# A two-layer diffusion backbone: row norms of the MLP summed in two halves, and low parts moved to another engine

## The chip, the cores and the metric

The kernel runs on one core of one Trainium2 chip. The metric is the device time of one execution in microseconds. The core's engines run side by side and are tied by semaphores: TensorE (PE in the profile) multiplies and transposes, VectorE (DVE) and ScalarE (ACT) work on tiles and read the accumulators, GpSimd (POOL) works on tiles in the core's memory, SyncE (SP) issues most loads.

## The reference

Two trunk layers work on 512 latent tokens and, in the first layer only, on 256 context tokens, all of width 1024. The part that the change touches is the second half of each layer:

```python
mix = concatenate([pool_mixer(...), gla_output(...), attention(...)]) @ w_out
x = x + ga1 * mix
x = x + ga2 * squared_relu_mlp(rmsnorm(x, g_mlp) * (1 + sc2) + sh2, w_up, w_down)

def rmsnorm(x, g):
    return x * rsqrt(mean(x * x, axis=-1) + 1e-6) * g
def squared_relu_mlp(h, w_up, w_down):
    return square(relu(h @ w_up)) @ w_down
```

The context tokens do the same with their own modulation. All is float32; a second norm of the same kind opens the next layer.

## The kernel before, in words

Every product is made of three fp32r passes: each operand is split into a high part (rounded) and a low part (the rest), and high x high, low x high and high x low are summed. Weights are loaded (`raw`), rounded on ScalarE (`whi`, line 159) and subtracted on VectorE (`wlo`, line 78). Tokens lie in tiles of 128 rows; two tiles are a pair. Layer 0 has six tiles (pairs 0 and 1 latent, pair 2 context), layer 1 four (pairs 0 and 1).

Behind the mixers a layer goes through the output projection (`op`, `tm_matmul`, line 335). Its first 512 columns are made for all tiles; each result is scaled on VectorE (`rtmp`, line 1157) and added to the residual `X` on GpSimd (line 1158). Then come the second 512 columns pair by pair, added to `X` on VectorE. While pair p is projected, `norm_pair(p-1)` norms the pair before:

- ScalarE squares the whole row of 1024 and sums it (line 270, a scratch write into `xn`), GpSimd makes rstd from the sum in two tiny steps (lines 252 and 253), VectorE scales the row into `xn` (line 280);
- TensorE transposes `xn` in blocks of 128 (line 287) into `ptr` banks, four blocks in one bank: column blocks k and k+1 of both tiles;
- per column block k (0 to 7) ScalarE writes the modulated high part `h2h` (line 295), VectorE or, for k = 1 and 5, ScalarE writes the same in full (`full`, lines 299 and 297), and the low part `h2l` is full less high (line 300): on GpSimd for even k, on VectorE for odd k.

The last pair is normed inside the first block of the MLP: `fm_pair` (line 325) multiplies the first column groups (two in layer 0, four in layer 1) pair by pair, the last pair's norm stands ahead of its own `fm_pair`. After that the up projection runs over whole token rows (`fm_matmul`, lines 316 and 318), `relu` on ScalarE and its square on VectorE follow, and the down projection (`dn`, line 335) comes a block of 512 hidden columns later. In layer 0 the MLP carries the modulation sums of layer 1 with it: weights `rawm` are loaded (line 222) and accumulated into `macc`, the first on ScalarE (line 226), the others on VectorE (line 228). At the end of layer 0 the same `norm_pair` makes the input `hT` of layer 1.

The pools decide much of the timing. The tag "full" has two buffers, "xn" has two (the `macc` tiles take theirs from this tag too). The order on each engine isn't written by hand: the tile framework simulates the program and fixes one static order for each engine, so an edit in one place moves instructions in others.

```python
xn = bp.tile([128, D], F32, tag=tag, name=nm(tag), bufs=2)
ss = mp.tile([128, 1], F32, tag="ss", name=nm("ss"))
A.activation(xn, xt, AF.Square, accum_out=ss)
...
full = bp.tile([128, 512], F32, tag="full", name=nm("full"), bufs=2)
...
(V if kk else G).tensor_tensor(lo, f, hi.bitcast(F32), ALU.subtract)
```

Of the kernel before, what the change touches and what calls it, by code (L numbers as in the profile page):

```python
# [10 lines left out]
F32 = mybir.dt.float32  # L11
F32R = mybir.dt.float32r
I32 = mybir.dt.int32
AF = mybir.ActivationFunctionType
ALU = mybir.AluOpType
AX = mybir.AxisListType

D = 1024
# [5 lines left out]
EPS = 1e-6  # L24
# [10 lines left out]
def hybrid_kernel(ctx, tc, x, c, cx, c_ctx, w_mod, b_mod, g_mix, w_in, w_pool, s_pool, w_gate, b_gate,  # L35
                  g_gla, g_q, g_k, w_out, g_mlp, w_up, w_down, g_final, k_mask, k_rope, k_edge, k_invw, out):
    nc = tc.nc
    V, A, G, T = nc.vector, nc.scalar, nc.gpsimd, nc.tensor

    const = ctx.enter_context(tc.tile_pool(name="const", bufs=1))  # L40
    lay = ctx.enter_context(tc.tile_pool(name="lay", bufs=1))
    wp = ctx.enter_context(tc.tile_pool(name="wp", bufs=5))
    sp = ctx.enter_context(tc.tile_pool(name="sp", bufs=29))
    mp = ctx.enter_context(tc.tile_pool(name="mp", bufs=2))
# [7 lines left out]
    def nm(s):  # L52
        uid[0] += 1
        return f"{s}_{uid[0]}"

    def slot(s, dt=F32, w=NT):
        return sp.tile([128, w], dt, tag="S", name=nm(s))
# [10 lines left out]
    def psA(s):  # L68
        return pa.tile([128, 1024], F32, tag="pa", name=nm(s))

    def psB(s):
        return pb.tile([128, 512], F32, tag="pb", name=nm(s))
# [21 lines left out]
    mhalf = const.tile([128, 1], F32, name="mhalf")  # L94
# [172 lines left out]
    def norm_rows(xt, tag="xn"):  # L267
        xn = bp.tile([128, D], F32, tag=tag, name=nm(tag), bufs=2)
        ss = mp.tile([128, 1], F32, tag="ss", name=nm("ss"))
        A.activation(xn, xt, AF.Square, accum_out=ss)  # L270
        return xn, rstd_of(ss, D, "rstd")

    def norm_pair(p2, X, hT, sc, sh, psf):

        pair = (2 * p2, 2 * p2 + 1)
        s = 0 if p2 < 2 else 1
        xns = []
        for t in pair:
            xn, r = norm_rows(X[t])
            V.tensor_scalar(xn, X[t], r, None, ALU.mult)  # L280
            xns.append(xn)
        col = pair[0] * 128
        for k2 in range(0, KT, 2):
            ps = psf("ptr")
            for kk in range(2):
                for i, xn in enumerate(xns):
                    T.transpose(ps[:, kk * 256 + i * 128:kk * 256 + (i + 1) * 128],
                                xn[:, (k2 + kk) * 128:(k2 + kk + 1) * 128], ident)
            full = bp.tile([128, 512], F32, tag="full", name=nm("full"), bufs=2)
            for kk in range(2):  # L290
                k = k2 + kk
                hi, lo = hT[k][0][:, col:col + 256], hT[k][1][:, col:col + 256]
                p_, f = ps[:, kk * 256:(kk + 1) * 256], full[:, kk * 256:(kk + 1) * 256]
                sc_, sh_ = sc[s][:, k:k + 1], sh[s][:, k:k + 1]
                A.activation(hi, p_, AF.Identity, scale=sc_, bias=sh_)
                if kk and k2 % 4 == 0:
                    A.activation(f, p_, AF.Identity, scale=sc_, bias=sh_)
                else:
                    V.tensor_scalar(f, p_, sc_, sh_, ALU.mult, ALU.add)
                (V if kk else G).tensor_tensor(lo, f, hi.bitcast(F32), ALU.subtract)  # L300

    def new_hT(s):
        return [(slot(s + "h", F32R), slot(s + "l", F32R)) for _ in range(KT)]
# [16 lines left out]
    def fm_pair(ps, wk, hT, nk, p2):  # L320

        cs = slice(p2 * 256, p2 * 256 + 256)
        for k in range(nk):
            for i, (a, b) in enumerate(passes(*wk(k), *hT[k])):
                T.matmul(ps[:, cs], a, b[:, cs], start=(k == 0 and i == 0), stop=(k == nk - 1 and i == 2))  # L325
# [91 lines left out]
    X = None  # L417
    MODS = [None, None]
    for l in range(2):
# [3 lines left out]
        live = alltiles if both else lat_tiles  # L423
# [4 lines left out]
        hT = hT1 if l else new_hT("hT")  # L428
        if l == 0:
            xstack = ExitStack()  # L430
            bp = xstack.enter_context(tc.tile_pool(name="np", bufs=1))
# [712 lines left out]
        bp = xstack.enter_context(tc.tile_pool(name=f"bp{l}", bufs=1))  # L1144
        X, XP = {}, {}
# [7 lines left out]
        def out_res(t, cb, ps):  # L1153

            sl = slice(cb * 512, (cb + 1) * 512)
            tmp = bp.tile([128, 512], F32, tag="rtmp", name=nm("rtmp"), bufs=2)
            V.tensor_tensor(tmp, ps, ga[0 if t < 4 else 1][:, sl], ALU.mult)
            (V if cb else G).tensor_tensor(X[t][:, sl], X[t][:, sl], tmp, ALU.add)
# [3 lines left out]
        for t in live:  # L1162
            ps = psB("op")
            tm_matmul(ps, t, wk, mixT, KT)
            out_res(t, 0, ps)
        h2 = new_hT("h2")
        msc, msh = [scT[:, 1, s] for s in range(2)], [shT[:, 1, s] for s in range(2)]
        wk = wcols(w_out[l], 512, 512, 4)
        for p2 in range(np_):
            ps = psA("op")  # L1170
            for i in range(2):
                tm_matmul(ps[:, i * 512:(i + 1) * 512], 2 * p2 + i, wk, mixT, KT)
                if p2 and i == 0:
                    norm_pair(p2 - 1, X, h2, msc, msh, psB)
                out_res(2 * p2 + i, 1, ps[:, i * 512:(i + 1) * 512])


# [32 lines left out]
        for b in range(NB):  # L1210
            act = []
            for i in range(4):
                nj = 2 if both else 4
                if b == 0 and i < nj:
                    if i == 0:
                        wks = [wcols(w_up[l], j * 128, 128, 1) for j in range(nj)]
                        pss = [psA("up") for j in range(2)]
                        if nj > 2:
                            pss = [p_[:, h * 512:h * 512 + 512] for p_ in pss for h in range(2)]
                        for p2 in range(np_):  # L1220
                            if p2 == np_ - 1:
                                norm_pair(p2, X, h2, msc, msh, psB)
                            for j in range(nj):
                                fm_pair(pss[j], wks[j], h2, KT, p2)
                    ps = pss[i]
                else:
                    wk = wcols(w_up[l], b * 512 + i * 128, 128, 1)
                    ps = psA("up")
                    fm_matmul(ps, wk, h2, KT, True, both)
                r_ = slot("relu")  # L1230
                A.activation(r_[:, 0:N_], ps[:, 0:N_], AF.Relu)  # L1231
                if b % 2 and i < 2:
                    w_ = wide("a", F32R)
                    ah, al = w_[:, 0:NT], w_[:, NT:2 * NT]
                else:
                    ah, al = slot("ah", F32R), slot("al", F32R)
                V.tensor_tensor(r_[:, 0:N_], r_[:, 0:N_], r_[:, 0:N_], ALU.mult)
                A.activation(ah[:, 0:N_], r_[:, 0:N_], AF.Copy)
                sub_lo(al[:, 0:N_], r_[:, 0:N_], ah[:, 0:N_])
                act.append((ah, al))  # L1240
                next(mods, None)
            if pend is not None:
                down(*pend)
            pend = (act, b)
        run(mods)
        if both:
            next_w = [wcols(w_in[1], c0, 128, 2, sl=True) for c0 in (256, 512)]
            hT1 = new_hT("hT")
            msc, msh = [MODS[1][1][:, 0, s] for s in range(2)], [MODS[1][2][:, 0, s] for s in range(2)]

            def after(t):
                if t in (2, 4, 5):
                    norm_pair((2, 4, 5).index(t), X, hT1, msc, msh, psB)

            down(*pend, after)
        else:

            gf = bp.tile([128, D], F32, tag="ga", name="gf", bufs=2)
            nc.scalar.dma_start(gf, g_final.partition_broadcast(128))
            halves = [slice(0, 512), slice(512, 1024)]  # L1260

            def after(t):
                y0, y1 = slot("y", w=512), slot("y", w=512)
                ss = mp.tile([128, 2], F32, tag="ssf", name=nm("ssf"))
                sq = bp.tile([128, 512], F32, tag="full", name=nm("sqf"), bufs=2)
                c0, c1 = halves
                for h, cs in enumerate(halves):
                    A.activation(sq, X[t][:, cs], AF.Square, accum_out=ss[:, h:h + 1])
                G.tensor_tensor(y0, X[t][:, c0], gf[:, c0], ALU.mult)
                G.tensor_tensor(ss[:, 0:1], ss[:, 0:1], ss[:, 1:2], ALU.add)  # L1270
                r = rstd_of(ss[:, 0:1], D, "rstd")
                A.activation(y0, y0, AF.Copy, scale=r)
                nc.scalar.dma_start(out[0, t * 128:(t + 1) * 128, c0], y0)
                V.scalar_tensor_tensor(y1, X[t][:, c1], r, gf[:, c1], ALU.mult, ALU.mult)
                nc.sync.dma_start(out[0, t * 128:(t + 1) * 128, c1], y1)

            down(*pend, after)

    xstack.close()
# [54 lines left out]
```

## Time and profile before

| | |
|---|---|
| median of three runs | 1677.33 us (1676.63 to 1677.76) |
| the profiled execution | 1673.25 us, its span 1671.5 us |
| granted TensorE clock, mean | 0.987 |
| TensorE busy | 1596.4 us (96%) |
| VectorE busy | 919.9 us (55%) |
| ScalarE busy | 632.4 us (38%) |
| GpSimd busy | 411.9 us (25%) |

A start in the trace is counted from the beginning of the span. The window 425 to 465 us holds the norms of pairs 1 and 2 of layer 0, 975 to 1022 the boundary between the layers, 1290 to 1340 the last norm and the first MLP block of layer 1. Instructions of one kind that follow each other are merged in a timeline row (x2 is two of them, and the time is that of both). A wait row says which engine waited, at which line, for whom, and for how long. The granted clock is 1.00 at 2.4 GHz and 0.50 at 1.2 GHz; a number between is a stretch that had both.

### The profile page before, as it was taken

Reading aid. Unit: us, or ns where it says so; the run is one execution under the profiler, and the core shown is the slowest. Engines: PE = TensorE matmul, PEld = TensorE weight load, DVE = VectorE, ACT = ScalarE, POOL = GpSimd, SP = SyncE. Lnnn points to the kernel's source line nnn. Section 1 sums busy time; section 2 is a strip of 40 time slices with the busy share of each in tenths; the row PEclk is TensorE's granted clock in tenths of the full one; section 3 lists DMA queues with packets and bytes.
Section 4 is the critical chain, followed back from the end, with each engine's and each line's share of the span. In section 5 each row is a group of like instructions: output and inputs, shape, how many; then the busy total and the mean of one; then the engine's idle time right before and its main releaser. Section 6 shows DMA issues by size and latency. Waiting matters only on the chain.

```text
span 1671.5 us, 27433 instructions
## 1 busy us (share of the span) xinstructions
PE 1596.4 (96%) x11403; PEld 1305.1 (78%) x11403; DVE 919.9 (55%) x1326; ACT 632.4 (38%) x1078; POOL 411.9 (25%) x484
## 2 busy tenths in 40 slices
PE   7999979899999999999999999897999899999997
PEld 4888756678888888888888889785667888888885
DVE  4437665753673654636446553587763645445554
ACT  5544445661531312213123234455662523223332
POOL 1121311212303041230321462242101122222225
PEclk9999989999999999999999999998999999999999
DMA  9445400222340422515324332100032313333321
GB/s 327 131 127 178 153 2 1 103 89 63 101 139 26 140 97 61 176 48 174 139 76 170 104 108 80 40 2 2 24 124 81 114 51 101 101 101 101 101 101 51
DMA packets 136636, 163.31 MB, mean 98 GB/s; under 512 B 9908, under 2 KB 108608, under 8 KB 136512
## 3 DMA queue, kind: packets, MB, share of 16 engines
q1 hardware_dynamic: 130176, 148.41, 27.9%
q10 hardware_dynamic: 5824, 13.12, 2.2%
q8 instruction: 89, 1.46, 0.4%
q14 instruction: 35, 0.29, 0.1%
q0 software_dynamic: 512, 0.03, 0.0%
HBM read 157.31 MB, written 4.23 MB: 97 GB/s over the span
## 4 chain that ended last, share of the span: by engine, by line
PE 84%; DVE 5%; ACT 4%; DMA 2%; issue 2%; POOL 2%; SPq 0%; ACTq 0%; POOLq 0%; DVEq 0%
PE dn L335 25%; PE up L316 19%; PE tm L335 7%; PE op L335 6%; PE up L318 5%; PE fm L316 4%; PE av L1066 3%; PE pT L1049 2%; PE up L325 2%; PE fm L318 2%; PE sc L1028 1%; PE att L764 1%; PE sc L1029 1%; PE pm L190 1%; DVE nmx L1031 1%
## 5 line engine op out<-in xcount | busy, mean ns | idle before, releaser
L159 ACT ACTIVATE whi<-raw 128x1024 fp32r<-128x1024 f32 (+2 forms) x182 | 185.1, 1031 | 567.2 <-PE dn L335 292.6
L1189 POOL TENSOR_TENSOR X<-X,rtmp 128x512 f32<-128x512 f32 x158 | 216.4, 1372 | 636.0 <-DVE rtmp L1188 635.7
L78 DVE TENSOR_TENSOR wlo<-raw,whi 128x1024 fp32r<-128x1024 f32 (+2 forms) x182 | 223.8, 1238 | 214.8 <-ACT whi L159 212.5
L1188 DVE TENSOR_TENSOR rtmp<-dn,ga 128x512 f32<-128x512 f32 x160 | 109.4, 688 | 215.4 <-PE dn L335 212.2
L335 PE MATMUL dn<-whi,ah 128*128 128x512 f32 x480 | 187.3, 390 | 0.0
L335 PE MATMUL dn<-whi,al 128*128 128x512 f32 x480 | 187.2, 390 | 0.0
L335 PE MATMUL dn<-wlo,ah 128*128 128x512 f32 x480 | 186.4, 390 | 0.0
L316 PE MATMUL up<-h2h,whi 128*128 128x512 f32 x464 | 182.5, 393 | 1.5 <-ACT relu L1231 1.5
L316 PE MATMUL up<-h2h,wlo 128*128 128x512 f32 x464 | 183.0, 394 | 0.0
L316 PE MATMUL up<-h2l,whi 128*128 128x512 f32 x464 | 182.7, 394 | 0.0
L335 PEld LDWEIGHTS dn<-whi,ah 128*128 128x128 f32 x480 | 90.1, 188 | 20.2 <-DVE rtmp L1188 0.8
L335 PEld LDWEIGHTS dn<-whi,al 128*128 128x128 f32 x480 | 90.1, 188 | 19.5
L316 PEld LDWEIGHTS up<-h2h,whi 128*128 128x128 f32 x464 | 87.1, 188 | 23.3 <-ACT relu L1231 1.7
L335 PEld LDWEIGHTS dn<-wlo,ah 128*128 128x128 f32 x480 | 90.1, 188 | 19.1
L316 PEld LDWEIGHTS up<-h2l,whi 128*128 128x128 f32 x464 | 87.1, 188 | 21.7 <-issue 2.5
L335 PE MATMUL tm<-whi,hTh 128*128 128x256 f32 (+1 forms) x352 | 102.2, 291 | 1.0 <-ACT UV L886 1.0
L316 PEld LDWEIGHTS up<-h2h,wlo 128*128 128x128 f32 x464 | 87.1, 188 | 19.6
L335 PE MATMUL tm<-whi,hTl 128*128 128x256 f32 (+1 forms) x352 | 100.7, 287 | 0.0
L335 PE MATMUL dn<-whi,a 128*128 128x512 f32 x320 | 99.9, 395 | 0.4 <-DVE rtmp L1188 0.4
L335 PE MATMUL tm<-wlo,hTh 128*128 128x256 f32 (+1 forms) x352 | 100.3, 288 | 0.0
L228 DVE SCALAR_TENSOR_TENSOR macc<-rawm,sstat,macc 128x1024 f32<-128x1024 f32 x56 | 76.1, 1379 | 9.3 <-DMA rawm<-in_w_mod_dram 8.7
L1031 DVE TENSOR_REDUCE nmx<-sc 128x1 f32<-128x768 f32 x64 | 60.4, 954 | 24.2 <-PE sc L1029 23.5
(295 smaller groups left out, 3324.9 us busy)
## 6 DMA issues: line engine op xcount, KB each, us to landing
rawm<-in_w_mod_dram SPq DMA_DIRECT2D x80, 512.0 KB, 4.9
raw<-in_w_up_dram SPq DMA_DIRECT2D x64, 512.0 KB, 4.6
raw<-in_w_down_dram SPq DMA_DIRECT2D x64, 512.0 KB, 4.6
raw<-in_w_in_dram SPq DMA_DIRECT2D x26, 512.0 KB, 3.9
rawm<-in_w_mod_dram SPq DMA_DIRECT2D x32, 256.0 KB, 5.3
raw<-in_w_out_dram SPq DMA_DIRECT2D x16, 512.0 KB, 4.5
raw<-in_w_in_dram SPq DMA_DIRECT2D x12, 256.0 KB, 3.0
ga<-gaD ACTq DMA_DIRECT2D x6, 512.0 KB
```

The lines of the kernel that those rows point to most:

```text
L78: V.tensor_tensor(lo, full, hi.bitcast(F32), ALU.subtract)
L159: A.activation(hi, raw, AF.Copy)
L228: V.scalar_tensor_tensor(acc[s], raw, c_, acc[s], ALU.mult, ALU.add)
L316: T.matmul(ps[:, 0:NL], a, b[:, 0:NL], start=st, stop=sp_)
L318: T.matmul(ps[:, NL:NT], a, b[:, NL:NT], start=st, stop=sp_)
L325: T.matmul(ps[:, cs], a, b[:, cs], start=(k == 0 and i == 0), stop=(k == nk - 1 and i == 2))
L335: T.matmul(ps, a[:, sl], bb, start=(k == 0 and i == 0), stop=(k == nk - 1 and i == 2))
L1031: V.tensor_reduce(nmx[:, i:i + 1], sv, AX.X, ALU.max, negate=True)
L1049: T.transpose(pt_[:, i * 128:(i + 1) * 128], p_[:, ki * 128:(ki + 1) * 128], ident)
L1066: T.matmul(av_[64 * hh:64 * hh + 64, 0:256], vst, pe[:, hh * 256:hh * 256 + 256], start=(ki == 1), stop=(ki == len(kts) - 2))
L1188: V.tensor_tensor(tmp, ps, ga[0 if t < 4 else 1][:, sl], ALU.mult)
L1189: (V if b == NB - 1 and not both and t == 3 else G).tensor_tensor(X[t][:, sl], X[t][:, sl], tmp, ALU.add)
```

## The change

Squares of a tile's first 512 columns are taken for all tiles right behind the first half of the output projection, into a tile of sums `ss0`. The MLP norms then square only the second 512 columns, and GpSimd adds both sums. Each half square is scaled by 1/32, so its sum is that of the mean. A half square writes its scratch into a tile of tag "full", no longer into `xn`. The norm at the boundary between the layers keeps its whole square. A flag `last` puts all eight low parts of a norm on VectorE; it is set for the last pair of the MLP norms in both layers, and for the last pair of the norm at the boundary.

```diff
-    def norm_pair(p2, X, hT, sc, sh, psf):
+    def half_square(xt, half, ss):
+
+        sq = bp.tile([128, 512], F32, tag="full", name=nm("sq"), bufs=2)
+        A.activation(sq, xt[:, half * 512:(half + 1) * 512], AF.Square, scale=1.0 / 32, accum_out=ss)
+
+    def norm_pair(p2, X, hT, sc, sh, psf, ss0=None, last=False):
...
-            xn, r = norm_rows(X[t])
+            if ss0 is None:
+                xn, r = norm_rows(X[t])
+            else:
+                xn = bp.tile([128, D], F32, tag="xn", name=nm("xn"), bufs=2)
+                ss = mp.tile([128, 1], F32, tag="ss", name=nm("ss"))
+                half_square(X[t], 1, ss)
+                r = mp.tile([128, 1], F32, tag="rstd", name=nm("rstd"))
+                G.tensor_scalar(r, ss, ss0[:, t:t + 1], EPS, ALU.add, ALU.add)
+                G.tensor_tensor(r, r, mhalf, ALU.pow)
...
-                (V if kk else G).tensor_tensor(lo, f, hi.bitcast(F32), ALU.subtract)
+                (V if kk or last else G).tensor_tensor(lo, f, hi.bitcast(F32), ALU.subtract)
...
             out_res(t, 0, ps)
+        ss0 = lay.tile([128, 6], F32, tag="ss0", name=nm("ss0"))
+        for t in live:
+            half_square(X[t], 0, ss0[:, t:t + 1])
...
-                    norm_pair(p2 - 1, X, h2, msc, msh, psB)
+                    norm_pair(p2 - 1, X, h2, msc, msh, psB, ss0)
...
-                                norm_pair(p2, X, h2, msc, msh, psB)
+                                norm_pair(p2, X, h2, msc, msh, psB, ss0, last=True)
...
-                    norm_pair((2, 4, 5).index(t), X, hT1, msc, msh, psB)
+                    norm_pair((2, 4, 5).index(t), X, hT1, msc, msh, psB, last=t == 5)
```

The orders move with it. ScalarE, layer 0, around the squares of pair 2 (X_4384 is the context pair, ptr_4833 and ptr_4850 hold blocks of pair 1, ptr_5042 and ptr_5061 those of pair 2); before:

```order
L297 ACTIVATE full_4838<-ptr_4833,shT_126,scT_125 128x256
L295 ACTIVATE h2h_4590<-ptr_4857,shT_126,scT_125 128x256
L270 ACTIVATE xn_5028,ss_5029<-X_4384 128x1024
L295 ACTIVATE h2h_4594<-ptr_4869,shT_126,scT_125 128x256
L270 ACTIVATE xn_5035,ss_5036<-X_4384 128x1024
L295 ACTIVATE h2h_4588<-ptr_4845,shT_126,scT_125 128x256
```

and with the change:

```order
L309 ACTIVATE h2h_4605<-ptr_4874,shT_126,scT_125 128x256
L311 ACTIVATE full_4879<-ptr_4874,shT_126,scT_125 128x256
L309 ACTIVATE h2h_4609<-ptr_4886,shT_126,scT_125 128x256
L276 ACTIVATE sq_5047,ss_5046<-X_4384 128x512
L276 ACTIVATE sq_5055,ss_5054<-X_4384 128x512
L309 ACTIVATE h2h_4595<-ptr_5061,shT_126,scT_125 128x256
```

The squares stood in the middle of pair 1's high parts and stand behind the last of them now. The first of the two half squares waits for the low parts k4 and k5 of pair 1, which free its buffer.

VectorE, layer 0, the end of pair 2 (h2l_4593 and h2l_4606 are the low part k5, h2l_4597 and h2l_4610 are k7, rawm_5286 and rawm_5305 the second load that the modulation sums take on VectorE); before:

```order
L228 SCALAR_TENSOR_TENSOR macc_5146<-rawm_5220,sstat,macc_5146 128x1024
L300 TENSOR_TENSOR h2l_4593<-full_5071,h2h_4592 128x256
L299 TENSOR_SCALAR full_5083<-ptr_5078,scT_125,shT_126 128x256
L300 TENSOR_TENSOR h2l_4597<-full_5083,h2h_4596 128x256
L228 SCALAR_TENSOR_TENSOR macc_5145<-rawm_5286,sstat,macc_5145 128x1024
L228 SCALAR_TENSOR_TENSOR macc_5146<-rawm_5286,sstat,macc_5146 128x1024
```

and with the change:

```order
L228 SCALAR_TENSOR_TENSOR macc_5165<-rawm_5239,sstat,macc_5165 128x1024
L314 TENSOR_TENSOR h2l_4608<-full_5102,h2h_4607 128x256
L314 TENSOR_TENSOR h2l_4606<-full_5090,h2h_4605 128x256
L313 TENSOR_SCALAR full_5102<-ptr_5097,scT_125,shT_126 128x256
L228 SCALAR_TENSOR_TENSOR macc_5164<-rawm_5305,sstat,macc_5164 128x1024
L314 TENSOR_TENSOR h2l_4610<-full_5102,h2h_4609 128x256
L228 SCALAR_TENSOR_TENSOR macc_5165<-rawm_5305,sstat,macc_5165 128x1024
```

A sum that needs the next load of modulation weights moved ahead of the last low part, and k6 (h2l_4608) is now VectorE's too.

TensorE, layer 1, the end of the pass over pairs (up_12526 and up_12556 are the last accumulator of the pass); before:

```order
L325 MATMUL up_12526<-h2l_12302,whi_12521 128x256
L325 MATMUL up_12526<-h2h_12301,wlo_12522 128x256
L316 MATMUL up_12815<-h2h_12287,whi_12811 128x512
L316 MATMUL up_12815<-h2l_12288,whi_12811 128x512
L316 MATMUL up_12815<-h2h_12287,wlo_12812 128x512
```

and with the change:

```order
L339 MATMUL up_12556<-h2l_12330,whi_12551 128x256
L339 MATMUL up_12556<-h2h_12329,wlo_12552 128x256
L349 MATMUL dn_13015<-whi_12993,ah_12815 128x512
L349 MATMUL dn_13031<-whi_12993,ah_12815 128x512
L349 MATMUL dn_13047<-whi_12993,ah_12815 128x512
L330 MATMUL up_12847<-h2h_12315,whi_12843 128x512
```

Three matmuls of the first down projection stood behind the next 24 `up` matmuls and stand ahead of them now.

## Rows read from the trace of the kernel before

**Rows 1.** The page: its first line, and the chain that ended last by engine.

```profile
span 1671.5 us, 27433 instructions
...
PE 84%; DVE 5%; ACT 4%; DMA 2%; issue 2%; POOL 2%; SPq 0%; ACTq 0%; POOLq 0%; DVEq 0%
```

**Rows 2.** Waits of TensorE, 425 to 465: total, times, longest, in us.

```profile
PE up L316 <- ACT relu L1231: 1.5, 1, 1.5
PE up L325 <- DVE h2l L300: 0.8, 1, 0.8
...
PE up L325 <- POOL h2l L300: 0.5, 1, 0.5
```

**Rows 3.** Waits of TensorE, 1290 to 1340.

```profile
PE up L325 <- POOL h2l L300: 2.0, 3, 1.3
PE up L325 <- ACT h2h L295: 1.1, 2, 0.6
...
PE ptr L287 <- DVE xn L280: 0.6, 1, 0.6
```

**Rows 4.** Waits of TensorE, 975 to 1022.

```profile
PE fm L325 <- POOL hTl L300: 0.7, 1, 0.7
```

**Rows 5.** Timeline of ScalarE, layer 0: start, duration (us), engine, line, what; idle before.

```profile
443.38 1.05 ACT L270 ACTIVATE xn<-X 128x1024 f32<-128x1024 f32 x1
...
448.74 1.93 ACT L295 ACTIVATE h2h<-ptr,shT,scT 128x256 fp32r<-128x256 f32 x4 [1.37 <-PE ptr L287]
...
454.78 1.15 ACT L226 ACTIVATE macc<-rawm,sstat 128x1024 f32<-128x1024 f32 x1
...
460.00 1.06 ACT L159 ACTIVATE whi<-raw 128x1024 fp32r<-128x1024 f32 x1 [2.71 <-PE up L325]
```

**Rows 6.** Instruction groups of ScalarE, 1600 to 1672: busy us, mean ns.

```profile
L1268 ACT ACTIVATE sqf<-X 128x512 f32<-128x512 f32 x8 | 5.0, 630 | 17.4 <-POOL X L1189 15.7 <-DVE X L1189 1.7
...
L1268 ACT ACTIVATION_READ_ACCUMULATOR sqf<-X 128x1 f32 x8 | 1.5, 186 | 0.0
```

**Rows 7.** Instruction groups of GpSimd, 361 to 470.

```profile
L300 POOL TENSOR_TENSOR h2l<-full,h2h 128x256 fp32r<-128x256 f32 x12 | 10.9, 916 | 22.1 <-DVE full L299 17.6 <-PE op L335 2.5 <-ACT h2h L295 1.9
```

**Rows 8.** Timeline of GpSimd, layer 0, pairs 1 and 2.

```profile
445.02 0.19 POOL L252 TENSOR_SCALAR rstd<-ss 128x1 f32<-128x1 f32 x1
445.29 0.55 POOL L253 TENSOR_TENSOR rstd<-rstd,mhalf 128x1 f32<-128x1 f32 x1
...
456.41 2.04 POOL L300 TENSOR_TENSOR h2l<-full,h2h 128x256 fp32r<-128x256 f32 x1 [2.01 <-DVE full L299]
```

**Rows 9.** Timeline of VectorE, layer 0, and (the last row) layer 1.

```profile
447.35 0.75 DVE L280 TENSOR_SCALAR xn<-X,rstd 128x1024 f32<-128x1024 f32 x1 [0.27 <-POOL rstd L253]
448.02 0.75 DVE L300 TENSOR_TENSOR h2l<-full,h2h 128x256 fp32r<-128x256 f32 x2
...
459.70 2.48 DVE L228 SCALAR_TENSOR_TENSOR macc<-rawm,sstat,macc 128x1024 f32<-128x1024 f32 x2 [0.93 <-DMA rawm<-in_w_mod_dram]
...
1324.46 1.23 DVE L78 TENSOR_TENSOR wlo<-raw,whi 128x1024 fp32r<-128x1024 f32 x1 [5.90 <-ACT whi L159]
```

**Rows 10.** Timeline of SyncE's DMA queue, layer 0: loads issued.

```profile
455.95 6.58 SPq L222 DMA_DIRECT2D rawm<-in_w_mod_dram  x3
```

**Rows 11.** Timeline of TensorE: next up group in layer 0, and in layer 1.

```profile
461.81 0.50 PE L316 MATMUL up<-h2h,whi 128*128 128x512 f32 x1 [1.49 <-ACT relu L1231]
...
1331.93 0.40 PE L316 MATMUL up<-h2h,whi 128*128 128x512 f32 x1
```

**Rows 12.** DMA issues by line: count, size, median us from issue to landing.

```profile
rawm<-in_w_mod_dram SPq DMA_DIRECT2D x80, 512.0 KB, 4.9
...
raw<-in_w_down_dram SPq DMA_DIRECT2D x64, 512.0 KB, 4.6
```

**Rows 13.** Stretches: length, busy us and count (PE, PEld, DVE, ACT, POOL), clock, DMA.

```profile
455.00:460.00 5.00, 4.17 (x33) 3.80 (x32) 4.04 (x7) 2.29 (x5) 2.04 (x1) 1.00 0.36 105
...
1300.00:1305.00 5.00, 3.28 (x16) 2.92 (x17) 2.47 (x4) 3.51 (x7) 1.77 (x2) 0.78 1.08 310
```

## The prediction

> **What bounds the kernel now.** I read the page's chain of waits first: TensorE holds 84% of the chain that ended last, in a span of 1671.5 us [rows 1]. So time is won or lost only where TensorE stands still, and a faster ScalarE or GpSimd is worth what it takes off such a stop. The list of TensorE's waits around the three norms that the change touches shows these stops. Around the last pair of layer 0 (window 425 to 465): 1.5 us for the relu that frees the next accumulator, 0.8 for a low part of VectorE, 0.5 for one of GpSimd [rows 2]. Around the last pair of layer 1 (1290 to 1340): 2.0 us in three waits for GpSimd's low parts, 1.1 for high parts of ScalarE, 0.6 for a scaled tile (xn) [rows 3]. At the boundary between the layers one such wait, 0.7 us, is for a low part of GpSimd [rows 4]. Together about 7 us could be had; that is the most the change can aim at. A difference under 0.2% (3.35 us) is about what a measurement of this kernel can't tell from no change.
>
> **What it adds and removes.** Ten squares of 128x1024 (1.05 us each, the first row of [rows 5]) become twenty of 128x512, whose nearest row is the final norm's own half squares: 0.63 us, and 0.19 for reading the sum [rows 6]. ScalarE gains 20 x 0.82 less 10 x 1.24, about 4 us of work, over two layers. Ten of the twenty stand at the first half of the output projection between weight conversions, where ScalarE idles much of the time; I cost them at nothing, and 0.35 us if they push a conversion that TensorE wants. The other ten are what stands on the path of each pair: 0.63 where 1.05 stood, 0.4 us sooner per square. GpSimd's two tiny steps stay two. Twelve low parts leave GpSimd (0.92 us each on the mean, 2.04 at worst [rows 7, 8]) for VectorE (two in 0.75 [rows 9]). No DMA is added.
>
> **Layer 0: the new wait.** The half squares write into the two "full" buffers, which the low parts read; the old squares wrote into xn. In the order of the changed kernel pair 1's squares stand behind the low parts k4 and k5 of pair 0, and pair 2's (the context pair, last) behind those of pair 1. Queued behind them on ScalarE is the last high part of the pair before, and behind those GpSimd's rstd, VectorE's xn, TensorE's transposes. Before, pair 2's squares went at 443.38 between the high parts of pair 1 [rows 5], and its second xn was scaled from 447.35 [rows 9]. Now: the low parts of VectorE that pair 1 waited for ended at 448.77 (448.02 and 0.75 [rows 9]); without two squares of 1.05 us among its high parts, but begun about 1 us later (its own squares wait too), and with a better placed order, I put that end at 446.5 to 447.4 (estimate from these rows). From there 0.54 + 0.63 + 0.19 for the squares, 0.19 + 0.55 on GpSimd [rows 8], 0.75 for xn and half a us for the first four transposes make 3.4 us; with a hop between engines each time the first high part of pair 2 starts at 450.3 to 451.2. It started at 448.74 [rows 5].
>
> From there ScalarE runs six high or full parts at 0.45 (four end to end in 1.93 [rows 5]), a macc, one more high part, and a macc of 1.15: some 5.7 us, so its second macc ends at 456.0 to 456.9, where it ended at 455.93 [rows 5]. That end releases the next load of modulation weights, which was issued at 455.95 [rows 10] and used from 459.70 [rows 9]: 3.75 us. In the new order the macc that waits for this load stands on VectorE **ahead of the last low part, k7**; before, k7 stood ahead of it. So k7 waits for a DMA: load at 459.8 to 460.7, macc 1.24 (half of the 2.48 for two [rows 9]), k7 0.4, end at 461.4 to 462.3. Behind that come the first matmul on k7's low part, 0.4 (the wide one of [rows 11] takes 0.50), and 1.81 from the weight conversion that waits for it over the relu to the next accumulator's first matmul (460.00 to 461.81 [rows 5, 11]). That gives 463.6 to 464.5 for what was at 461.81 [rows 11]: **+1.8 to +2.7, taken +2.4**, nearer the upper end since 3.75 us is under the median for such loads [rows 12]. Outer ends: nothing, if the load lands early enough or the squares go sooner; +4.0, if the load takes that median, 4.9 us.
>
> The four low parts on VectorE (4 x 0.38) lie inside this wait, since VectorE has to stop for the load anyway; I add nothing for them. VectorE was busy 4.04 of 5 us in the stretch 455 to 460 [rows 13]. The Trainium skill (Perfetto Trace Analysis, Optimizing Scalar/DVE Operations) advises the opposite direction, moving work off VectorE where it is saturated, even to GpSimd; by that the four would come on top, and the sum would be 1.5 us longer.
>
> **Boundary.** The low part k0 that TensorE waited for comes on VectorE behind two full parts, at about the time at which GpSimd delivered it; the rest there is bound by ScalarE's high parts. Zero, between -0.7 (the whole wait [rows 4]) and +0.5.
>
> **Layer 1: a gain given back.** Pair 1's squares no longer stand among pair 0's high parts, and TensorE's order has all four column groups of pair 0 ahead of pair 1's transposes. Of the 3.7 us of waits [rows 3] some 1.1 comes back as a wait for k0's low part (VectorE now makes all eight), and 0.3 for other small ones: the pass ends 2.3 us sooner. But three `dn` matmuls now stand ahead of the next `up` group, which before followed the pass directly, at 1331.93 [rows 11]. They wait for a weight of the down projection. Its load goes out when VectorE has split the weight two before it (1324.46 + 1.23 [rows 9]); the column group that frees that buffer ends 51 matmuls before the pass's end where it was 73, so the split ends at about 1326.0 in spite of the earlier pass; with 4.6 us to land [rows 12] the load is there at 1330.6, by the 3.75 seen above at 1329.8. The conversion (1.04) and the high part behind it (0.6) make TensorE's start 1331.4 to 1332.2, the pass having ended at 1329.7. Three dn matmuls (0.68) are then already done, and the next group starts at 1332.1 to 1332.9, against 1331.93 + 0.68: **-0.5 to +0.3, taken -0.2**; -2.3 if the load is early. Small moves in layer 1's attention: nothing, +/-1.
>
> **Sum.** +2.4 + 0 - 0.2 = +2.2 us. The profiled execution took 1673.25 us around its span of 1671.5; the median of the runs is 1677.33, 4.1 above. The durations are of the former, the sum is laid on the latter: **1679.5 us**.
>
> **Rivals.**
> - *The layer 1 gain stays* (faster). If the down weight lands before the pass ends, 2.3 us stay. The clock adds to it: granted 0.78 in the stretch 1300 to 1305 [rows 13], so 44% of it at 1.2 GHz instead of 2.4, among the very waits that go; its 0.22 x 5 = 1.1 us are won too. With layer 0 at zero: 1677.33 - 2.3 - 1.1 = 1673.9; with layer 0 as forecast 1676.3. For it: 3.7 us of waits really are removed. Against: the position of the dn matmuls. Over 0.2% faster needs nearly all of it: chance 0.15.
> - *TensorE's clock falls in layer 0* (slower). The stretch 455 to 460 kept 1.00 with 0.8 us of waits in it, while 1300 to 1305, behind waits of at most 1.25, got 0.78 [rows 13]. Between 450 and 464 the new order stops TensorE for 5 us or so where it was 3. The rival decides once the stops before k7 pass those of layer 1's bad stretch; the price is 1.1 us for such a stretch: 1680.6, and with the load at 4.9 us (1.15 longer) 1681.8. The Trainium skill (TensorE: Matmul & The Clock Gate, What's actually happening) has the clock follow how busy the engine has lately been; the row of 0.78 agrees. Chance of over 0.2% slower, by this and the late load: 0.28.
> - *The edits don't reach the path* (no change). Squares, low parts and the late load could all hide behind TensorE's own order, and the time stays at 1677.3. This lies within 0.2%, as does the forecast: 0.57 together, the forecast about 0.4 of it.
>
> **How the numbers follow.** The range takes the first rival with the forecast's layer 0 half undone (1676.3 - 1.2) at the low end, and at the high end layer 0 at its outer +4.0 with the clock's 1.1 on top: 1675.1 to 1682.2. Beyond it lie the full gain of layer 1 with nothing lost, and both losses at their outer ends, about 1 in 10 each.
>
> **What would show it.** Right: pair 2's squares of layer 0 start about 447, the first high part behind them past 450; the list of waits has a low part of VectorE above 1 us there, and VectorE idles for a load of modulation weights right ahead of it; the next `up` group starts about 464; GpSimd's low parts are gone from the waits of layer 1, and `dn` waits 1.5 to 2.5 us for ScalarE. Wrong: if k7 doesn't wait, if the squares of pair 2 aren't late, if `dn` doesn't wait, or if a stretch outside these three places moves by over 1 us.

## The result, and the profile after

The changed kernel is slower: 1683.86 us in the median of ten runs (1681.82 to 1685.68) against 1675.99 for the kernel before on the same chip (ten runs). The ratio is 1.0051, with a 95% interval of 1.0040 to 1.0061: 8.5 us, between 6.7 and 10.2 (the two medians differ by 7.9; further on, a difference in us that stands beside a ratio is worked out from the ratio). The forecast was 1679.5, with a range that ended at 1682.2. The profiled execution of the change took 1684.77 us, its span is 1683.0, 11.5 above the span profiled before. The two traces lie further apart than the medians, since the kernel before was profiled in one of its faster executions (1673.25 us).

The page of the changed kernel, its first line, TensorE's busy time and the chain that ended last:

```profile
span 1683.0 us, 27436 instructions
PE 1603.3 (95%) x11403; PEld 1311.6 (78%) x11403; DVE 926.1 (55%) x1338; ACT 637.5 (38%) x1098; POOL 405.5 (24%) x472
PE 83%; DVE 6%; ACT 4%; DMA 3%; POOL 2%; issue 2%; ACTq 0%; SPq 0%; POOLq 0%; DVEq 0%
```

TensorE runs the same 11403 matmuls and still carries the chain [rows 1]. It is busy 6.9 us longer with the same work, and stands still for the rest of the difference.

**Where the time went.** The start of the same instruction in both traces gives a lag, and the stages in which the lag grows are the ones that lost time. It is 0.9 us before the output projection of layer 0 (the same kernel profiled twice differs there by 1.9), 8.6 from 554 us to the end of layer 0 and still 8.6 behind the boundary norm. In layer 1 then 1.2 come on behind a wait for `QQ`, ahead of the attention, 1.6 in the attention and 0.3 in its norm and first MLP block. So layer 0's norms cost 7.7 us, the boundary nothing, layer 1's norm almost nothing, and two stretches that the change doesn't name cost 2.8.

**Layer 0: pair 1 lost its lead.** ScalarE of the changed kernel around pairs 1 and 2 (timeline: start, duration, engine, line, what, idle before):

```profile
438.34 0.63 ACT L276 ACTIVATE sq<-X 128x512 f32<-128x512 f32 x1
...
445.00 1.21 ACT L309 ACTIVATE h2h<-ptr,shT,scT 128x256 fp32r<-128x256 f32 x2 [4.00 <-PE ptr L301]
...
451.07 0.63 ACT L276 ACTIVATE sq<-X 128x512 f32<-128x512 f32 x1
...
455.96 1.93 ACT L309 ACTIVATE h2h<-ptr,shT,scT 128x256 fp32r<-128x256 f32 x4 [3.40 <-PE ptr L301]
...
460.80 1.14 ACT L226 ACTIVATE macc<-rawm,sstat 128x1024 f32<-128x1024 f32 x1
```

Pair 1's squares begin at 438.34, behind pair 0's high parts. Before, they were done by 432, as ScalarE and VectorE of the kernel before show:

```profile
429.88 1.05 ACT L270 ACTIVATE xn<-X 128x1024 f32<-128x1024 f32 x1
...
440.51 1.02 ACT L295 ACTIVATE h2h<-ptr,shT,scT 128x256 fp32r<-128x256 f32 x2 [2.01 <-PE ptr L287]
```

```profile
432.19 0.75 DVE L280 TENSOR_SCALAR xn<-X,rstd 128x1024 f32<-128x1024 f32 x1
433.38 0.75 DVE L280 TENSOR_SCALAR xn<-X,rstd 128x1024 f32<-128x1024 f32 x1 [0.45 <-POOL rstd L253]
```

There both tiles of pair 1 were scaled by 434.13 and its first high part came at 440.51, so 6.4 us of lead lay between. The change spends all of it and 4.5 us more (0.7 of them lag that was there at 430 us): the first high part is at 445.00. From there all is as late: pair 2's squares at 451.07 (443.38 in [rows 5]), its first high part at 455.96 (448.74), ScalarE's second macc.

**Layer 0: the norm's chain on GpSimd.** GpSimd and VectorE of the changed kernel:

```profile
439.16 0.87 POOL L292 TENSOR_SCALAR rstd<-ss,ss 128x1 f32<-128x1 f32 x1 [3.27 <-ACT sq L276]
440.11 0.56 POOL L293 TENSOR_TENSOR rstd<-rstd,mhalf 128x1 f32<-128x1 f32 x1
440.77 0.86 POOL L292 TENSOR_SCALAR rstd<-ss,ss 128x1 f32<-128x1 f32 x1
441.71 0.57 POOL L293 TENSOR_TENSOR rstd<-rstd,mhalf 128x1 f32<-128x1 f32 x1
442.24 0.72 POOL L314 TENSOR_TENSOR h2l<-full,h2h 128x256 fp32r<-128x256 f32 x1
...
453.02 0.86 POOL L292 TENSOR_SCALAR rstd<-ss,ss 128x1 f32<-128x1 f32 x1
```

```profile
440.71 0.75 DVE L294 TENSOR_SCALAR xn<-X,rstd 128x1024 f32<-128x1024 f32 x1 [0.31 <-POOL rstd L293]
442.31 1.21 DVE L294 TENSOR_SCALAR xn<-X,rstd 128x1024 f32<-128x1024 f32 x1 [0.85 <-POOL rstd L293]
...
452.96 0.75 DVE L294 TENSOR_SCALAR xn<-X,rstd 128x1024 f32<-128x1024 f32 x1 [0.85 <-POOL rstd L293]
454.56 0.75 DVE L294 TENSOR_SCALAR xn<-X,rstd 128x1024 f32<-128x1024 f32 x1 [0.85 <-POOL rstd L293]
...
465.93 1.28 DVE L228 SCALAR_TENSOR_TENSOR macc<-rawm,sstat,macc 128x1024 f32<-128x1024 f32 x1 [1.40 <-DMA rawm<-in_w_mod_dram]
467.13 0.42 DVE L314 TENSOR_TENSOR h2l<-full,h2h 128x256 fp32r<-128x256 f32 x1
```

GpSimd's four tiny steps for a pair take 3.1 us (439.16 to 442.28), and the last low part of pair 0 that was left on GpSimd (442.24) stands behind them; TensorE waits 1.0 us for it. The first step, 0.19 us on one operand [rows 8], has a second operand now: its shortest times are 0.30, and 0.86 where an xn of VectorE runs beside it (the 0.87 at 439.16 stands beside a `wlo` and an `X`). The step on one operand was not always short either: in the kernel before the one at 446.10, beside the xn that began at 445.87, took 0.58. The two rows of 0.86 here end at 441.63 and 453.88, each 0.17 behind the end of the xn that began just ahead of it (441.46 and 453.71). The Trainium skill (SBUF — State Buffer, Who interferes with whom) says that VectorE and GpSimd share a port pair, and that where VectorE's instruction runs in a two-port mode, which a `tensor_scalar` can enter, the one that issues first holds the pair for the whole instruction while the other blocks; these two rows agree. The xn at 442.31, which takes 1.21 us instead of 0.75 beside a low part that GpSimd began at 442.24, would fit the other direction.

At the end of pair 2 k7 waits as foreseen: the sum ahead of it on VectorE starts at 465.93 after 1.40 us of idle for its load, which SyncE issued at 461.97, behind ScalarE's macc, 3.96 us before (3.75 before the change). TensorE's waits from 425 to 475 (total, times, longest, in us):

```profile
PE up L339 <- DVE h2l L314: 3.8, 3, 1.8
PE ptr L301 <- DVE xn L294: 2.1, 3, 1.0
PE up L330 <- ACT relu L1248: 1.5, 1, 1.5
PE up L339 <- POOL h2l L314: 1.0, 1, 1.0
PE up L339 <- ACT h2h L309: 0.4, 1, 0.4
PE up L339 <- DVE rtmp L1171: 0.4, 1, 0.4
```

They sum to 9.2 us. The same window held 4.2 before (the three of [rows 2] and 1.4 in smaller ones): 5.0 us of the 7.7.

**Layer 0: the clock.** The rest is TensorE's granted clock, in stretches of the changed kernel (length, busy us and count of PE, PEld, DVE, ACT, POOL, then the clock):

```profile
440.00:442.50 2.50, 1.24 (x9) 0.82 (x8) 1.34 (x3) 0.57 (x1) 2.24 (x5) 1.00 1.06 340
442.50:445.00 2.50, 1.98 (x11) 1.98 (x12) 1.90 (x3) 0.00 (x0) 0.47 (x1) 0.69 0.97 298
445.00:447.50 2.50, 2.50 (x15) 2.44 (x13) 1.09 (x2) 2.13 (x5) 1.27 (x2) 0.62 0.02 6
...
465.00:467.50 2.50, 0.83 (x7) 0.63 (x6) 1.57 (x3) 0.00 (x0) 0.00 (x0) 1.00 0.01 5
467.50:470.00 2.50, 0.91 (x5) 0.70 (x6) 2.13 (x3) 1.97 (x3) 0.00 (x0) 1.00 0.13 16
470.00:472.50 2.50, 2.50 (x11) 2.12 (x12) 2.50 (x4) 1.99 (x3) 0.00 (x0) 0.65 0.90 313
472.50:475.00 2.50, 2.50 (x12) 2.12 (x12) 1.77 (x2) 0.29 (x1) 0.00 (x0) 0.66 1.06 335
```

Twice TensorE stands still for half of a stretch or more, and then runs part of the next 5 us at 1.2 GHz: first behind its waits for pair 1's xn and pair 0's low part, then behind k7 and the relu. Before, all of 425 to 475 had 1.00. Busy time times what the clock lacks of 1.00 gives an estimate of the loss: 1.98 x 0.31 + 2.50 x 0.38 = 1.6 us, and 2.50 x 0.35 + 2.50 x 0.34 = 1.7. The second can be seen directly: the next `up` group starts at 469.84, 8.0 us behind 461.81 [rows 11], and the fourth matmul of its kind behind it (466.15 before) at 475.68, 9.5 behind. With 3.3 us of clock on the 5.0 of waits, 8.3 us are accounted for; the lag, over a longer stretch, says 7.7.

**Layer 1.** TensorE's waits from 1290 to 1350 in the changed kernel:

```profile
PE up L339 <- POOL h2l L314: 1.7, 2, 1.2
PE dn L349 <- ACT ah L1255: 1.6, 1, 1.6
PE op L349 <- DVE rtmp L1171: 1.1, 1, 1.1
PE up L339 <- DVE h2l L314: 0.9, 1, 0.9
PE up L339 <- ACT h2h L309: 0.6, 1, 0.6
```

The `dn` matmuls wait 1.6 us that they didn't wait before, as foreseen. But GpSimd's low parts keep 1.7 of the 2.0 us of [rows 3]: those waits are for pair 0, which the flag doesn't touch.

In the attention TensorE's waits are no longer than before (1080 to 1210: 14.3 us in all, 14.9 before). What differs is the clock. The same window of the kernel before, and of the changed one (which is some 10 us behind, so the work in it is an earlier part):

```profile
1190.00:1200.00 10.00, 9.75 (x88) 6.79 (x88) 9.41 (x16) 4.31 (x9) 1.19 (x4) 1.00 0.01 3
```

```profile
1190.00:1200.00 10.00, 8.90 (x70) 7.20 (x69) 5.43 (x14) 4.92 (x9) 0.00 (x0) 0.66 0.01 2
```

Summed as above over all of 1080 to 1210, the clock took 3.3 us before and 7.4 with the change.

The 1.2 us ahead of the attention are the clock's too. TensorE waits 3.4 us for `QQ` in both kernels; the 10 us behind that wait, before and with the change:

```profile
1067.00:1077.00 10.00, 8.80 (x154) 7.03 (x155) 6.90 (x15) 5.33 (x13) 2.29 (x6) 0.83 0.20 55
```

```profile
1075.60:1085.60 10.00, 9.69 (x152) 7.60 (x152) 5.74 (x13) 4.14 (x7) 2.28 (x6) 0.69 0.20 53
```

No build edits anything there. Run 6 below kept 1.00 at this place and gained 1.4 us on the kernel before.

### The profile page after: what moved, and what is told of

It reads as the page before. It is cut to its first block, busy times and chain, and to the rows that moved or that the text cites. A ratio compares the mean times of both kernels' runs of the same rounds, so it can differ in the third digit from the quotient of the medians.

```text
span 1683.0 us, 27436 instructions
## 1 busy us (share of the span) xinstructions
PE 1603.3 (95%) x11403; PEld 1311.6 (78%) x11403; DVE 926.1 (55%) x1338; ACT 637.5 (38%) x1098; POOL 405.5 (24%) x472
## 4 chain that ended last, share of the span: by engine, by line
PE 83%; DVE 6%; ACT 4%; DMA 3%; POOL 2%; issue 2%; ACTq 0%; SPq 0%; POOLq 0%; DVEq 0%
PE dn L349 25%; PE up L330 19%; PE tm L349 7%; PE op L349 6%; PE up L332 5%; PE fm L330 4%; PE av L1080 3%; PE pT L1063 2%; PE fm L332 1%; PE up L339 1%; PE sc L1042 1%; PE att L778 1%; PE sc L1043 1%; DVE nmx L1045 1%; PE pm L190 1%
## 5 line engine op out<-in xcount | busy, mean ns | idle before, releaser
L228 DVE SCALAR_TENSOR_TENSOR macc<-rawm,sstat,macc 128x1024 f32<-128x1024 f32 x56 | 74.4, 1347 | 11.5 <-DMA rawm<-in_w_mod_dram 10.8
```

The costliest lines, as they stand in the source:

```text
L228: V.scalar_tensor_tensor(acc[s], raw, c_, acc[s], ALU.mult, ALU.add)
```

## Experiments

Two theories were set against each other for layer 0: the half squares, whose scratch now lies in the buffers of "full", come late (theory A), or the low parts on VectorE, with k7 behind a load, make the loss (theory B). A third question was the loss in layer 1's attention: does it come from the order there, which an edit elsewhere can move (theory R)? Each expectation names the theories that it sets apart.

The table sums up what the sections below use. The ratio is to the kernel before; "waits" and "clock" are TensorE's in 425 to 475, the clock's loss estimated as above; "attention" is what the clock took in 1080 to 1210.

| kernel | ratio (95%) | waits | clock | attention |
|---|---|---|---|---|
| before | 1 | 4.2 | 0.0 | 3.3 |
| the change | 1.0051 (1.0040 to 1.0061) | 9.2 | 3.3 | 7.4 |
| 1: low parts back | 1.0030 (1.0020 to 1.0041) | 7.8 | 1.5 | 4.5 |
| 2: low parts only | 1.0027 (1.0015 to 1.0038) | 7.3 | 1.6 | 6.3 |
| 3: squares in xn | 0.9999 (0.9986 to 1.0011) | 5.1 | 1.6 | 6.4 |
| 4: 3, low parts back | 0.9999 (0.9986 to 1.0012) | 5.2 | 0.0 | 6.5 |
| 5: before again | one run | 4.3 | 0.0 | 4.8 |
| 6: layer 1 only | 1.0003 (0.9989 to 1.0016) | 4.2 | 0.0 | 3.2 |
| 7: sum on VectorE | 1.0044 (1.0031 to 1.0058) | 7.2 | 1.6 | 6.3 |
| 8: 4 and 7 | 0.9985 (0.9975 to 0.9995) | 3.4 | 0.0 | 4.9 |
| 9: 3 and 7 | 1.0015 (1.0003 to 1.0027) | 6.3 | 1.5 | 4.9 |

**1. The low parts back on GpSimd.** The change without its flag:

```diff
-                (V if kk or last else G).tensor_tensor(lo, f, hi.bitcast(F32), ALU.subtract)
+                (V if kk else G).tensor_tensor(lo, f, hi.bitcast(F32), ALU.subtract)
```

> The changed kernel with all even low parts of the last pairs back on GpSimd (the flag has no effect); half squares stay in the 'full' buffers. Theory A (the half squares wait for 'full' buffers, so pair 2 of layer 0 starts late; the flag costs only what k7 waits for the modulation load): still 4.5 to 7 us slower than before, pair 2's squares start after 449 and its first high part after 454, k7 does not wait for a load. Theory B (the low parts on VectorE are what costs): within 2 us of before, pair 2's first high part back under 451.

1679.76 us, 5.0 slower than before. The first high part of pair 2 stays late (455.00) and the lag that layer 0 adds is 5.7 us where the change adds 7.7, so in the traces the half squares alone do most of the damage. k7 is ahead of the macc again, and the second fall of the clock is gone: 1.00 from 457.5 to 477.5, where the change had 0.65; the first, behind pair 1's xn, is still there.

**2. The low parts alone.** The kernel before with the flag:

```diff
-    def norm_pair(p2, X, hT, sc, sh, psf):
+    def norm_pair(p2, X, hT, sc, sh, psf, last=False):
...
-                (V if kk else G).tensor_tensor(lo, f, hi.bitcast(F32), ALU.subtract)
+                (V if kk or last else G).tensor_tensor(lo, f, hi.bitcast(F32), ALU.subtract)
...
-                                norm_pair(p2, X, h2, msc, msh, psB)
+                                norm_pair(p2, X, h2, msc, msh, psB, last=True)
...
-                    norm_pair((2, 4, 5).index(t), X, hT1, msc, msh, psB)
+                    norm_pair((2, 4, 5).index(t), X, hT1, msc, msh, psB, last=t == 5)
```

> The kernel before with only the flag: last pairs' low parts all on VectorE, whole squares as before. Theory A: pair 2's squares and first high part where they were before (443.4 and 448.7, within 1), but in this order k7 stands behind both sums on the late load, so the next up group starts 3 to 5 us later; whole time 2 to 5 us slower than before. Theory B: 6 us slower or more.

1679.74 us, 4.5 slower by itself. The first high part of pair 2 is hardly late (449.15), but both sums on VectorE stand ahead of k7 and wait for the load. VectorE, then TensorE's list of waits (425 to 475), in this kernel:

```profile
459.93 2.48 DVE L228 SCALAR_TENSOR_TENSOR macc<-rawm,sstat,macc 128x1024 f32<-128x1024 f32 x2 [0.92 <-DMA rawm<-in_w_mod_dram]
```

```profile
PE up L325 <- DVE h2l L300: 3.6, 2, 2.5
```

k7 costs 2.5 us here, and behind it the clock falls, the second place of the change (0.56 in 465 to 467.5), but not at the first. So runs 1 and 2 each hold one of the change's two falls, and the change holds both. Their losses by the ratios, 5.0 and 4.5 us, sum to no more than the 8.5 of both together within the intervals. In the traces they overlap: each adds waits to layer 0, 3.6 and 3.1 us, and both together 5.0.

**3 and 4. The squares' scratch in "xn".** With the flag (3), and without it (4):

```diff
-    def half_square(xt, half, ss):
+    def half_square(xt, half, ss, xn=None):
 
-        sq = bp.tile([128, 512], F32, tag="full", name=nm("sq"), bufs=2)
-        A.activation(sq, xt[:, half * 512:(half + 1) * 512], AF.Square, scale=1.0 / 32, accum_out=ss)
+        xn = bp.tile([128, D], F32, tag="xn", name=nm("sq"), bufs=2) if xn is None else xn
+        A.activation(xn[:, 0:512], xt[:, half * 512:(half + 1) * 512], AF.Square, scale=1.0 / 32, accum_out=ss)
...
-                half_square(X[t], 1, ss)
+                half_square(X[t], 1, ss, xn)
```

> The changed kernel with the half squares' scratch in xn buffers in place of 'full' buffers; all else as changed, the flag too. Theory A: pair 2's squares go before 446 and its first high part by 450, k7 ahead of the late load; the time is within 2 us of before, 6 us or more under the changed kernel. Theory B: the low parts still cost, 5 us slower than before.

> As e3, with the flag off as in e1: only the half squares are left of the change, with their scratch in xn. Theory A: 3 us faster to 1 slower than before, like e3 within 2 us. Theory B: at before's time, 5 us under e3.

1674.47 and 1674.63 us, both the time of before. ScalarE of run 4, pair 2's squares among pair 1's high parts once more:

```profile
442.48 0.62 ACT L276 ACTIVATE xn<-X 128x512 f32<-128x512 f32 x1
...
443.99 0.63 ACT L276 ACTIVATE xn<-X 128x512 f32<-128x512 f32 x1
```

Pair 1's tiles are scaled at 431 to 434 in both, as before the change; in the change and in run 1 they are at 439 to 444. The place of a scratch that nobody reads moves them. That shows theory A. Layer 0 is won back (the lag that it adds is +1.3 us in run 3 and -1.2 in run 4), the attention's 1.6 us are not. The clock's first fall is gone in both. A later one is there in run 3 (0.57 in 462.5 to 465) and not in run 4:

```profile
462.50:465.00 2.50, 2.50 (x17) 2.21 (x16) 2.50 (x3) 0.76 (x2) 0.00 (x0) 1.00 0.66 203
```

Yet TensorE's last two waits ahead of it are alike, 0.84 us for a low part of VectorE and 1.49 for the relu in run 3, 0.89 and 1.50 in run 4, and k7 stands ahead of the load in both. So this fall is not the flag's price, and what sets the two traces apart is not shown. The medians, 0.2 us apart, agree: in this order, with k7 ahead of the load, no price of the flag is seen.

**5. The kernel before, profiled again.** No edit; it shows how far two traces of one kernel differ.

> The kernel before, unchanged, for a second profile. Theory R (all variants so far carry the same other order in layer 1's attention, and it costs 1.6 us there): this run keeps the old order, so TensorE's clock is 1.00 in the stretch 1180 to 1200 as in the first profile and that stretch is as long as there. Theory C (chance of the run): the clock there is as low as 0.83, as in the changed kernel.

Span 1671.0 us. The lag moves by up to 2 us before the output projection, by 0.4 in layer 1's attention, where the clock took 4.8 us instead of 3.3, and by 0.6 in its norm and first block. So of a 1.6 us loss in the attention about 0.4 may be a trace's own scatter, and the 0.3 in the norm all of it.

**6. Layer 1 alone.** The half squares and the flag in layer 1 only:

```diff
-        ss0 = lay.tile([128, 6], F32, tag="ss0", name=nm("ss0"))
-        for t in live:
+        ss0 = None if both else lay.tile([128, 6], F32, tag="ss0", name=nm("ss0"))
+        for t in (() if both else live):
...
-                                norm_pair(p2, X, h2, msc, msh, psB, ss0, last=True)
+                                norm_pair(p2, X, h2, msc, msh, psB, ss0, last=not both)
...
-                    norm_pair((2, 4, 5).index(t), X, hT1, msc, msh, psB, last=t == 5)
+                    norm_pair((2, 4, 5).index(t), X, hT1, msc, msh, psB)
```

> The change in layer 1 alone (half squares and flag there, layer 0 and the boundary as before); the order up to layer 1's output projection is that of before. Theory R: no loss in layer 1's attention (0 within 0.4); the last norm with the three early dn matmuls is worth -0.5 to +0.5; total within 1 us of before. Rival: the layer 1 part is a gain of 2 us that the late start hid, total 2 us faster; or the loss in the attention comes back with any build.

1675.1 us, no difference. The `dn` wait of 1.6 us is there, and the lag grows by 0.3 us in the norm and first block, as expected: the gain in layer 1 is given back in full. The attention keeps its order and its time (+0.2). Outside both, 1.4 us are gained behind the wait for `QQ`, and 0.9 lost at the first matmul of the output projection, which waits 1.75 us for ScalarE's `pe` instead of 0.84; no cause is shown for that wait.

**7. The sum of the two halves on VectorE.** The change, with GpSimd left only the power:

```diff
-                G.tensor_scalar(r, ss, ss0[:, t:t + 1], EPS, ALU.add, ALU.add)
+                V.tensor_scalar(r, ss, ss0[:, t:t + 1], EPS, ALU.add, ALU.add)
```

> The changed kernel with the sum of the two halves on VectorE; GpSimd has only the power step of each rstd. The order of pair 2 of layer 0 is that of the changed kernel. Theory G (the two rstd in a row on GpSimd, 0.86 for the step with two operands, make about a third of the late start): the first high part of pair 2 starts 2 us earlier than in the changed kernel or more (its lag over the attention's end taken off), total 2 to 3 us under the changed kernel. Theory A alone (only the place of the squares counts): under 1 us gained.

VectorE and GpSimd of this kernel, pair 2:

```profile
448.51 0.20 DVE L292 TENSOR_SCALAR rstd<-ss,ss 128x1 f32<-128x1 f32 x1
```

```profile
448.86 1.38 POOL L293 TENSOR_TENSOR rstd<-rstd,mhalf 128x1 f32<-128x1 f32 x2 [0.81 <-DVE rstd L292]
```

The step is 0.20 us on VectorE. Pair 2's first high part comes at 451.66, 4.1 behind its squares (4.9 in the change). In the trace layer 0 loses 4.5 us instead of 7.7, and the clock's first fall (440 to 450) is gone. The median says less: 1682.07, a ratio of 1.0044 whose interval overlaps that of the change, where 2 to 3 us of gain were expected. The edit also moved something else: pair 1's squares stand further ahead in ScalarE's order (434.80 and 436.82, between pair 0's last high parts, where the change has 438.34 and 439.09). So GpSimd's steps have a part in pair 2's chain, and how much of layer 0's loss is theirs stays open.

**8 and 9. Together.** Scratch in "xn" and the sum on VectorE, without the flag (8) and with it (9); their edits are those of 3 and 7, and of 1 for run 8.

> As e4 (half squares with scratch in xn, low parts where they were before), and the sum of the halves on VectorE as in e7. If the late squares and the two-operand step were the losses of the half squares, what is left should gain in layer 0: 2 to 4 us less there than before (e4: 1.6), nothing in layer 1's norm, and the other order in layer 1's attention takes 1.6 back: 0 to 2 us faster than before in all. If the half squares bring nothing by themselves: within 0.5 of e4 in layer 0.

> As e8 with the flag on. Here k7 of layer 0 stands behind both sums on the late load (as in e2), and layer 1's attention stands nearly in the order of before (one state update moved). If the wait of k7 is the flag's price: 3 to 5 us more in layer 0 than e8. If the attention's order is what costs 1.6 in the others: 0 within 0.4 there and a clock of 1.00 throughout its last 40 us; if any build other than before loses it: 1.1 or more again.

Run 8 has the lowest ratio: 1673.2 us against 1674.74, 0.9985 (0.9975 to 0.9995), 2.5 us faster (1.5 by the medians), which is less than the 0.2% below which the prediction called a difference too small to tell. In the trace layer 0 gains 1.7 us, a little under the 2 to 4 expected, and layer 1's norm 1.2. TensorE's waits around its last pair of layer 0:

```profile
PE up L330 <- ACT relu L1248: 1.5, 1, 1.5
PE up L339 <- DVE h2l L314: 1.2, 1, 1.2
PE ptr L301 <- ACT full L311: 0.4, 1, 0.4
PE ptr L301 <- DVE xn L294: 0.3, 1, 0.3
```

They are 3.4 us where the kernel before had 4.2, at a clock of 1.00 throughout. Run 9 differs from it by the flag alone and is 5.0 us slower by the two ratios (0.9985 and 1.0015), 3.9 by the medians, and 3.5 by the lags that layer 0 adds. Its VectorE, and TensorE's clock behind it:

```profile
457.55 2.48 DVE L228 SCALAR_TENSOR_TENSOR macc<-rawm,sstat,macc 128x1024 f32<-128x1024 f32 x2 [1.17 <-DMA rawm<-in_w_mod_dram]
```

```profile
462.50:465.00 2.50, 2.13 (x7) 1.84 (x8) 1.93 (x2) 0.85 (x2) 0.00 (x0) 0.54 0.87 318
465.00:467.50 2.50, 2.50 (x13) 2.14 (x13) 0.94 (x1) 1.01 (x2) 0.00 (x0) 0.78 1.06 340
```

The flag's price in layer 0, k7 behind the load and the clock behind k7, stands here with the squares early: waits 6.3 against 3.4, clock 1.5 against 0. It is paid where the order puts k7 behind the load, in the change and in runs 2, 7 and 9, and not in run 3.

Run 9 also weakens theory R. Its order in the attention is close to that of before, and still 1.1 us are lost there, with the clock at 0.91 in 1160 to 1180 (run 5, the kernel before itself, has 0.91 there too and lost 0.4). Each build whose layer 0 was edited lost 0.9 to 1.7 us in the attention; the two whose layer 0 is that of before lost 0.2 and 0.4. The larger of these losses go with more time at the lower clock (6.3 to 7.4 us in the table's last column, against 3.2 to 4.8 in before, run 5 and run 6); in runs 1, 8 and 9 it is at the level of run 5, and no cause is shown for their 0.9 to 1.1. Whether the order there or the moment at which the stage begins sets the clock stays open.

## Why the prediction was wrong

- **The step that failed** is, in layer 0: "but begun about 1 us later (its own squares wait too)", and with it "the first high part of pair 2 starts at 450.3 to 451.2". Pair 1 began 4.5 us later (445.00 against 440.51), and pair 2's first high part came at 455.96. I had looked at what stood behind pair 1's squares in the new order, and not at when they ran before: at 429.88, with 6.4 us of lead, which was the cover that the tag took away. Runs 3 and 4 show it: with the scratch back in "xn", the lead is back.
- **"make 3.4 us"**, from the squares to the first high part, some 3.8 with the hops between engines, was 4.9. I timed one tile's chain. The bank that the high part reads holds both tiles of the pair, and the second xn starts 1.60 us behind the first (454.56 and 452.96), since GpSimd makes the two rstd one after the other and its step with two operands takes 0.39 and 0.86 here instead of the 0.19 that I put. In run 7 the same way takes 4.1.
- **The price behind it** was right: from the second macc's end to the next `up` group I had 7.6 us (456.0 to 463.6), measured 7.9 (461.94 to 469.84). The load, 3.75 put, took 3.96; k7's wait, the idle VectorE and the relu are all there. Nearly the whole excess up to that group entered with the late start.
- **The second rival came true on top of the forecast.** The clock fell in layer 0, at two places and not one, for 3.3 us and not 1.1. Its price was named on top of the forecast, as a rival with a chance of its own, and left out of the sum. Part of this is a trace's chance: run 3 and run 4 differ by such a fall behind the same waits.
- **Boundary**: right, 0 within 0.1 us.
- **Layer 1's norm**: right, +0.3 where -0.5 to +0.3 was given, and by the `dn` wait. One reason was wrong: GpSimd's low parts did not leave its waits, which are for pair 0.
- **"Small moves in layer 1's attention: nothing, +/-1"**: 1.6, at the lower clock, and 1.2 more ahead of it. These are stretches outside the three places, which the prediction named as a sign of error.
- **The low parts on VectorE at nothing**: right as far as it can be read. Ahead of k7 TensorE waits for two of VectorE's low parts of pair 2, 0.87 and 1.19 us; at the same two places run 1 waits 0.88 for GpSimd's and 1.45 for VectorE's.
- **The first squares at nothing**: right for the six of layer 0. In 361 to 440 the list of groups has 29.0 us of idle ahead of ScalarE's ten half squares, 15.2 of it for GpSimd's `X`, which is the first half, and the lag is no larger at 437 us than at 360.

So by this pair of traces 7.7 + 0 + 0.3 + 1.6 + 1.2 = 10.8 us stand where +2.2 was forecast; the timed runs say 8.5. The difference is the trace of before. Its mean granted clock is 0.987, where 35 other executions of that kernel have 0.984 on the mean (0.978 to 0.988), and the ten of the change 0.983. Span times what the mean clock lacks of 1.00 gives an estimate of 29.1 us for the change and 26.5 for the kernel before: on the mean of the runs the clock takes some 2.6 us of the loss, in this pair of traces more, and the waits take the rest.

## What to carry to other kernels

Before you price a step that moves behind another, read how early it ran and how long its result lay unused: a scratch tile's tag can take away that lead though nobody reads the tile. Where several tiles feed one bank, price the last tile's chain, on the engine that makes them in turn. And leave room for the clock behind each wait that you forecast on TensorE: two groups of waits of the change were followed by a loss of 1.6 and 1.7 us at the lower clock, though in runs 3 and 4 the same waits cost 1.6 us in one and nothing in the other.

## What was not expected of the hardware

- GpSimd's step on 128x1 is 0.19 us with one operand (0.58 at 446.10 of the kernel before, beside an xn of VectorE), 0.30 with a second per-partition one and, in the change, up to 0.87 beside VectorE; VectorE does the same in 0.20.
- The clock's price doesn't follow from the waits alone: a wait of 0.8 us for a low part with the relu's 1.5 behind it cost no clock in the kernel before [rows 2] and in run 4, and 1.6 us in run 3. k7's of 1.8 (the change) and 2.5 us (run 2), with the relu's 1.5 and 1.7 behind them, cost 1.7 and 1.6 us.
- In layer 1's attention, where no instruction was edited, the lower clock took between 3.2 and 7.4 us in the builds, and 3.3 and 4.8 in two profiles of the same kernel.
